# One-hot tiles of a gate-matrix builder: from four tokens innermost to one token after the other

## The chip, the cores and the metric

The kernel runs on one core of a Trainium2 chip. The metric is the device time of one execution, in microseconds (us). A profiled execution also leaves a trace of all five engines: TensorE (PE, with its weight loads listed apart as PEld), VectorE (DVE), ScalarE (ACT), GpSimd (POOL) and SyncE (SP, which issues most DMAs).

## The reference, cut to what matters

One layer of a decoder: three gated branches (dilated attention, a convolution module, attention into a memory), then a mixer called PEER that retrieves single-neuron experts. The prompt has 1024 tokens, the sample batch 8. Per token and head, PEER takes the best 16 of 128 keys on each of two sides, sums the pairs, and keeps 16 experts of the 128 x 128, so a token has 8 x 16 = 128 slots, each with a pair of indices and a softmax weight:

```
e = take_along_axis(i1, ci // 16) * 128 + take_along_axis(i2, ci % 16)
g = softmax(sc)
a = einsum('bd,bed->be', xb, u_tab[e])
out = einsum('be,bed->bd', g * gelu(a), v_tab[e])
```

## The kernel before, in words

The 1024 prompt tokens are treated in two ways. For the first 640 (five blocks of 128) the kernel runs all 16384 experts densely: it computes gelu(h u) for every expert and multiplies by a matrix G that holds the softmax weight where the token chose the expert and zero elsewhere. For the last 384 tokens and the samples it gathers the chosen rows of the tables by indirect DMA (`peer_gather`) and works on DVE.

The stages in order of the program: memory keys; `front(0)` (projections, attention, convolution and gates of the first 512 tokens); `tail` "0" (output projection, norm, top-k); then `front(1)` for the second 512 tokens, into which the G matrices of blocks 0 to 3 are woven by `gate_build`; the tails "1a" and "1b", with the G matrix of block 4 woven in; and last `peer_dense`, with the gather running beside it on POOL, the DMA queues and DVE.

`gate_build` makes G as a product of one-hots. A block's indices and weights are transposed, so that slots lie on the 128 partitions and tokens along the free dimension (`igT`). They are converted to f16 in the tile `ig`, whose four planes are first index, second index, weight times 16384, and what the rounding of that weight left over. Per batch of 8 tokens (TB = 8) DVE runs four operations of 1024 f16 elements: `o1` (first index equal to 0..127), `o2` (second index equal to 0..127), `wh` = o1 times weight, and `wl` = o1 times remainder, written over o1. In the trace and in the order all of them are called `oh`, on lines L1047, L1048, L1049 and L1051. Per token PE then runs two 128 x 128 matmuls into the PSUM tile `pG`: o2 is the stationary operand, wh (L1056) and wl (L1057) the moving one. Four tokens share a pG tile; ACT copies it into the staging tile `stg` (L1058), and after 32 tokens one DMA stores stg (`gscr`). There are 80 batches, 320 DVE operations, 160 pG tiles and 1280 matmuls.

Memory layout before: a one-hot tile is [128 partitions, TB/4, 128, 4], so the four tokens of a group lie side by side and the 128 elements of one token lie four elements (8 bytes) apart. The constant `iotaT` repeats each of 0..127 four times. So DVE reads all operands in runs of four neighbours, and PE reads its operands of one token with a step of four elements.

Every engine executes its instructions in the order of its queue. The order is made before the run by a scheduler that places instructions by priority and by an estimate of their durations. `gate_build` gets its priorities spread over `front(1)` (`prio0 + step * prio_step`), so its work is filled in between the matmuls of that stage. The one-hot tiles have two buffers per name, pG two, stg two, ig one.

Of the kernel before, what the change touches and what calls it, by code (L numbers as in the profile page):

```python
# [12 lines left out]
F16 = mybir.dt.float16  # L13
# [3 lines left out]
OP = mybir.AluOpType  # L17
# [4 lines left out]
P = 128  # L22
# [13 lines left out]
GSCALE = 16384.0  # L36
# [10 lines left out]
def peer_trunk(tc, I, O):  # L47
    nc = tc.nc
# [10 lines left out]
    with contextlib.ExitStack() as es:  # L59
# [12 lines left out]
        bkeep = es.enter_context(tc.tile_pool(name="bkeep", bufs=1, side="right"))  # L72
# [21 lines left out]
        def cload(name, shape, src=None, pool=None):  # L94
            t = (pool or const).tile(shape, F32, name=f"c_{name}", tag=f"c_{name}")
            prio = tc.cur_priority
            tc.cur_priority = prio + 300
            nc.sync.dma_start(t, I[name] if src is None else src)
            tc.cur_priority = prio
            return t  # L100
# [23 lines left out]
        iota = cload("iota", [P, P])  # L124
        iota16 = const.tile([P, TOPK], BF16, name="iota16", tag="iota16")
        nc.vector.tensor_copy(iota16, iota[:, 0:TOPK])
        iotaT = bkeep.tile([P, P, 4], F16, name="iotaT", tag="iotaT")
        nc.vector.tensor_copy(iotaT, iota.unsqueeze(2).to_broadcast([P, P, 4]))
        blk = cload("blk", [P, NS])
        sel = cload("sel", [32, NS])  # L130
        subk = cload("sub_keys", [P, 2, P])
# [15 lines left out]
        igT = {b: igp.tile([P, 3, P], F32, name=f"igT{b}") for b in range(4)}  # L147
# [868 lines left out]
        def gate_build(gb, pgs, toks, TB, prio0=None, prio_step=0):  # L1016

            step = 0
            for t0 in range(toks[0], toks[1], TC):
                bi = t0 // P  # L1020
                if t0 % P == 0:
                    pt = pgs.tile([P, 4, P], F32, tag="pG", bufs=2, name=f"igT{bi}")
                    for q in range(3):
                        nc.tensor.transpose(pt[:, q], igT[bi][:, q], ident)
                    nc.scalar.copy(igT[bi], pt[:, 0:3])
                    ig = gb.tile([P, 4, P], F16, tag="ig", bufs=2 if TB == 16 else 1, name=f"ig{bi}")
                    nc.vector.tensor_copy(ig[:, 0:2], igT[bi][:, 0:2])
                    nc.vector.tensor_scalar(ig[:, 2], igT[bi][:, 2], GSCALE, None, op0=OP.mult)
                    nc.vector.scalar_tensor_tensor(
                        ig[:, 3], igT[bi][:, 2], GSCALE, ig[:, 2], op0=OP.mult, op1=OP.subtract  # L1030
                    )
                stg = gb.tile([P, P, TC], F32, tag="stg", bufs=2, name=f"stg{t0}")
                for tb in range(0, TC, TB):
                    ts_ = slice(t0 % P + tb, t0 % P + tb + TB)
                    if prio0 is not None:
                        tc.cur_priority = prio0 + step * prio_step
                        step += TB // 4
                    o1, o2, wh = (
                        gb.tile([P, TB // 4, P, 4], F16, tag=f"oh{q}", bufs=2, name=f"oh{q}_{t0}_{tb}") for q in range(3)
                    )  # L1040
                    ioB = iotaT.unsqueeze(1).to_broadcast([P, TB // 4, P, 4])

                    def cols(q):
                        c = ig[:, q, ts_].rearrange("p (a t) -> p a t", t=4)
                        return c.unsqueeze(2).to_broadcast([P, TB // 4, P, 4])

                    nc.vector.tensor_tensor(o1, ioB, cols(0), op=OP.is_equal)  # L1047
                    nc.vector.tensor_tensor(o2, ioB, cols(1), op=OP.is_equal)  # L1048
                    nc.vector.tensor_tensor(wh, o1, cols(2), op=OP.mult)  # L1049
                    wl = o1  # L1050
                    nc.vector.tensor_tensor(wl, o1, cols(3), op=OP.mult)  # L1051
                    for t4 in range(0, TB, 4):
                        pG = pgs.tile([P, 4, P], F32, tag="pG", bufs=2, name=f"pG{t0}_{tb + t4}")
                        for t in range(t4, t4 + 4):
                            a, q = t // 4, t % 4
                            nc.tensor.matmul(pG[:, q], o2[:, a, :, q], wh[:, a, :, q], start=True, stop=False)  # L1056
                            nc.tensor.matmul(pG[:, q], o2[:, a, :, q], wl[:, a, :, q], start=False, stop=True)  # L1057
                        nc.scalar.activation(  # L1058
                            stg[:, :, tb + t4 : tb + t4 + 4], pG.rearrange("p t i -> p i t"), AF.Copy, scale=1.0 / GSCALE
                        )  # L1060
                nc.sync.dma_start(gscr[t0 // TC], stg)
# [66 lines left out]
        with tc.tile_pool(name="keep", bufs=1) as keep, tc.tile_pool(name="wts", bufs=1) as wp:  # L1128
            mem_stage(wp)
            mg = front(0, keep, wp)  # L1130
            p0 = tc.cur_priority + 2200
            tail("0", keep, wp, *mg, [(b * P, P, b * P) for b in range(4)] + [(HALF, NS, SEQ)])
            tc.cur_priority = p0
            phase.update(mm=3, o=1, g=2)
            with tc.tile_pool(name="psG", bufs=1, space=PSUM) as pgs:
                base = tc.cur_priority
                with tc.tile_pool(name="gb0", bufs=1, side="right") as gb:
                    gate_build(gb, pgs, (0, HALF), 8, base, 20)
                tc.cur_priority = base
                mg = front(1, keep, wp)  # L1140
                fes.close()
                gp = es.enter_context(tc.tile_pool(name="gath", bufs=1, side="right"))
                base = tc.cur_priority
                tc.cur_priority = base + low_prio
                peer_gather(gp, [gp], [NGB])
                gprio, tc.cur_priority = tc.cur_priority, base
                with (
                    tc.tile_pool(name="igp1", bufs=1, side="right") as igp1,
                    tc.tile_pool(name="topk1", bufs=1, side="right") as kp,
                    tc.tile_pool(name="gb1", bufs=1, side="right") as gb,  # L1150
                ):
                    igT[4] = igp1.tile([P, 3, P], F32, name="igT4")
                    tail(
                        "1a", keep, wp, *mg, [(b * P, P, HALF + b * P) for b in (0, 1)],
                        after=lambda b: gate_build(gb, pgs, (b * P, b * P + P), 8), kpool=kp,
                    )
                    tail("1b", keep, wp, *mg, [(b * P, P, HALF + b * P) for b in (2, 3)], kpool=kp)
# [88 lines left out]
```

## Time and profile before

| what | value |
|---|---|
| time, median of three runs | 3703.09 us (3703.05 to 3704.65) |
| profiled execution | 3695.24 us |
| its span, first to last instruction | 3693.1 us |
| PE matmul busy | 3429.9 us (93%) |
| PE weight loads busy | 3011.5 us (82%) |
| DVE busy | 2899.1 us (78%) |
| ACT busy | 1499.6 us (41%) |
| POOL busy | 565.7 us (15%) |
| mean granted TensorE clock | 0.961 of full speed |

Busy shares are averages over the whole span. The gate matrices of blocks 0 to 3 are built from about 1020 to 1500 us and that of block 4 from about 1725 to 1832 us; the dense stage follows to the end. Matmul records overlap (a matmul's record is longer than the time until the next one starts), so the time that a matmul costs in a row of matmuls is read from the starts of neighbours, not from the record's length.

### The profile page before, as it was taken

How to read it: one execution, taken by the hardware profiler on the slowest of the kernel's cores; microseconds unless marked ns; L12 is line 12 of the kernel's file. 1: busy time of each engine (PE TensorE's matmuls, PEld its weight loads, DVE VectorE, ACT ScalarE, POOL GpSimd, SP SyncE). 2: the span in 40 equal slices, each digit the busy share in tenths (PEclk: the TensorE clock that was granted, in tenths of full speed). 3: DMA queues.
4: the chain of work that ended last, by engine and by line, in shares of the span. 5: the costliest groups of instructions: out<-in, count | busy, mean ns of one | idle time of the engine just before them, and what ended most of it. 6: DMA issues, size and time to landing. Idle time of an engine off the chain costs nothing.

```text
span 3693.1 us, 55182 instructions
## 1 busy us (share of the span) xinstructions
PE 3429.9 (93%) x19969; PEld 3011.5 (82%) x19969; DVE 2899.1 (78%) x6275; ACT 1499.6 (41%) x3519; POOL 565.7 (15%) x398
## 2 busy tenths in 40 slices
PE   8987999898889989887899999999999999999998
PEld 6766989697677778676798888888989888898987
DVE  4358555499998656779988888887988888798988
ACT  6553552235755554344443333332333333233332
POOL 0000000000000000000012323322323332233332
PEclk9997999999999999998799999999999999999999
DMA  5467455423355546753668988888988988888987
GB/s 180 136 199 259 154 184 183 154 86 119 103 186 189 177 157 211 246 188 131 224 233 314 338 312 330 310 318 309 336 328 324 342 315 304 308 327 318 334 329 279
DMA packets 338454, 902.09 MB, mean 244 GB/s; under 512 B 32588, under 2 KB 140276, under 8 KB 285436
## 3 DMA queue, kind: packets, MB, share of 16 engines
q1 hardware_dynamic: 281732, 487.49, 39.7%
q0 software_dynamic: 56448, 411.07, 29.2%
q8 instruction: 157, 2.57, 0.3%
q14 instruction: 117, 0.96, 0.1%
HBM read 804.09 MB, written 94.83 MB: 243 GB/s over the span
## 4 chain that ended last, share of the span: by engine, by line
PE 31%; issue 30%; DVE 14%; DMA 13%; POOL 11%; ACT 2%; SPq 0%; POOLq 0%; DVEq 0%; ACTq 0%
POOL uv L981 11%; DMA uv<-in_uv,idxB 4%; PE pg L175 2%; PE pg L174 2%; PE pg L176 2%; PE pG L1057 2%; PE pG L1056 2%; DMA vr<-in_v_tab 1%; PE p_q L175 1%; PE p_q L176 1%; DMA wko<-kscr 1%; PE p_q L174 1%; DMA uv<-in_uv,idxS 1%; PE pa L174 1%; PE pa L176 1%
## 5 line engine op out<-in xcount | busy, mean ns | idle before, releaser
L981 POOL DMA_INDIRECT uv<-in_uv,idxB x384 | 555.8, 1448 | 1553.2 <-DVE gacc L995 1226.1
L174 PE MATMUL pa<-h2Ah,uh 128*128 128x320 f32 x2048 | 633.7, 310 | 2.2 <-ACT uh L158 2.2
L176 PE MATMUL pa<-h2Ah,ul 128*128 128x320 f32 x2048 | 631.9, 310 | 2.3 <-DVE ul L159 2.2
L175 PE MATMUL pa<-h2Al,uh 128*128 128x320 f32 x2048 | 633.2, 309 | 0.0
L985 DVE CUSTOM_DVE_ANT_0 uv<-uv,gh 128x1024 f32<-128x1024 f32 x392 | 478.5, 1222 | 138.2 <-DMA uv<-in_uv,idxB 119.9
L174 PE MATMUL pv<-vh,hh 128*128 128x512 f32 x1280 | 480.5, 396 | 44.3 <-ACT vh L158 28.4
L995 DVE SCALAR_TENSOR_TENSOR gacc<-uv,av,gacc 128x1024 f32<-128x1024 f32 x392 | 502.5, 1282 | 17.5 <-ACT av L993 12.6
L175 PE MATMUL pv<-vl,hh 128*128 128x512 f32 x1280 | 505.2, 395 | 9.3 <-DVE vl L159 9.3
L176 PE MATMUL pv<-vh,hl 128*128 128x512 f32 x1280 | 499.9, 393 | 0.0
L174 PEld LDWEIGHTS pa<-h2Ah,uh 128*128 128x128 f32 x2048 | 385.7, 188 | 6.9 <-ACT uh L158 2.4
L176 PEld LDWEIGHTS pa<-h2Ah,ul 128*128 128x128 f32 x2048 | 385.1, 188 | 5.4 <-DVE ul L159 2.8
L175 PEld LDWEIGHTS pa<-h2Al,uh 128*128 128x128 f32 x2048 | 385.4, 188 | 3.3 <-issue 0.9
L158 ACT CAST vh<-vr 128x512 fp32r<-128x512 f32 x256 | 157.2, 619 | 422.0 <-DMA vr<-in_v_tab 238.1
L174 PEld LDWEIGHTS pv<-vh,hh 128*128 128x128 f32 x1280 | 242.7, 190 | 99.0 <-ACT vh L158 40.0
L175 PEld LDWEIGHTS pv<-vl,hh 128*128 128x128 f32 x1280 | 243.6, 190 | 61.0 <-DVE vl L159 12.9
L176 PEld LDWEIGHTS pv<-vh,hl 128*128 128x128 f32 x1280 | 243.4, 190 | 50.0
L981 POOL DMA_INDIRECT uv<-in_uv,idxS x8 | 9.2, 1149 | 1556.3 <-ACT co L739 1513.2
L159 DVE TENSOR_TENSOR vl<-vr,vh 128x512 fp32r<-128x512 f32 x256 | 175.6, 688 | 77.0 <-ACT vh L158 76.5
L174 PE MATMUL pg<-hTh,wh_g 128*128 128x260 f32 (+1 forms) x576 | 192.9, 335 | 0.0
L175 PE MATMUL pg<-hTl,wh_g 128*128 128x260 f32 (+1 forms) x576 | 192.4, 334 | 0.0
L176 PE MATMUL pg<-hTh,wl_g 128*128 128x260 f32 (+1 forms) x576 | 192.3, 334 | 0.0
L990 ACT ACTIVATE av<-av 128x2 f32<-128x2 f32 x196 | 39.9, 204 | 375.3 <-DVE av L985 374.8
(558 smaller groups left out, 7651.3 us busy)
## 6 DMA issues: line engine op xcount, KB each, us to landing
ur<-in_uT SPq DMA_DIRECT2D x128, 512.0 KB
vr<-in_v_tab SPq DMA_DIRECT2D x256, 256.0 KB
gscr<-stg SPq DMA_DIRECT2D x20, 2048.0 KB
Gt<-gscr SPq DMA_DIRECT2D x32, 1280.0 KB
wr_g<-in_w_col SPq DMA_DIRECT2D x48, 512.0 KB
wr_q<-in_w_in SPq DMA_DIRECT2D x24, 512.0 KB
wr_u<-in_w_col SPq DMA_DIRECT2D x16, 512.0 KB
wr_pq<-in_w_col SPq DMA_DIRECT2D x16, 512.0 KB
```

Source lines behind the costliest of these rows:

```text
L158: nc.scalar.copy(hi, raw)
L159: nc.vector.tensor_tensor(lo, raw, hi.bitcast(F32), op=OP.subtract)
L174: nc.tensor.matmul(out, ah, bh, start=start, stop=False)
L175: nc.tensor.matmul(out, ah, bl, start=False, stop=False)
L176: nc.tensor.matmul(out, al, bh, start=False, stop=stop)
L981: nc.gpsimd.indirect_dma_start(out=uv, out_offset=None, in_=I["uv"], in_offset=bass.IndirectOffsetOnAxis(ap=col, axis=0),)
L985: nc.vector.tensor_tensor_reduce(out=uv[:, 0:D], in0=uv[:, 0:D], in1=h2, scale=1.0, scalar=0.0, op0=OP.mult, op1=OP.add, accum_out=av[:, s ...
L990: nc.scalar.activation(av, av, AF.Gelu_apprx_tanh)
L995: nc.vector.scalar_tensor_tensor(acc, uv[:, D:], av[:, j : j + 1], acc, op0=OP.mult, op1=OP.add)
L1056: nc.tensor.matmul(pG[:, q], o2[:, a, :, q], wh[:, a, :, q], start=True, stop=False)
L1057: nc.tensor.matmul(pG[:, q], o2[:, a, :, q], wl[:, a, :, q], start=False, stop=True)
```

## The change

One-hot tiles become [128 partitions, TB, 64, 2]: each token's 128 elements lie side by side, split into 64 pairs only so that an operand can be described in pairs. `ig` now holds every value twice in a row, and its two values are read 64 times per token; `iotaT` becomes plain 0..127, read once per token. The conversion into `ig` was one cast of two planes, one scaled copy and one subtraction; it is now two casts (one per plane), one scaled copy and one subtraction, each of 256 elements where a plane had 128. PE reads its operands without a step. Number, size and operands of the one-hot operations, matmuls and evacuations are as before.

```
-        iotaT = bkeep.tile([P, P, 4], F16, name="iotaT", tag="iotaT")
-        nc.vector.tensor_copy(iotaT, iota.unsqueeze(2).to_broadcast([P, P, 4]))
+        iotaT = bkeep.tile([P, P], F16, name="iotaT", tag="iotaT")
+        nc.vector.tensor_copy(iotaT, iota)
...
-                    ig = gb.tile([P, 4, P], F16, tag="ig", bufs=2 if TB == 16 else 1, name=f"ig{bi}")
-                    nc.vector.tensor_copy(ig[:, 0:2], igT[bi][:, 0:2])
-                    nc.vector.tensor_scalar(ig[:, 2], igT[bi][:, 2], GSCALE, None, op0=OP.mult)
+                    ig = gb.tile([P, 4, P, 2], F16, tag="ig", bufs=1, name=f"ig{bi}")
+
+                    def twice(q):
+                        return igT[bi][:, q].unsqueeze(2).to_broadcast([P, P, 2])
+
+                    for q in range(2):
+                        nc.vector.tensor_copy(ig[:, q], twice(q))
+                    nc.vector.tensor_scalar(ig[:, 2], twice(2), GSCALE, None, op0=OP.mult)
...
-                        gb.tile([P, TB // 4, P, 4], F16, tag=f"oh{q}", bufs=2, name=f"oh{q}_{t0}_{tb}") for q in range(3)
-                    )
-                    ioB = iotaT.unsqueeze(1).to_broadcast([P, TB // 4, P, 4])
+                        gb.tile([P, TB, P // 2, 2], F16, tag=f"oh{q}", bufs=2, name=f"oh{q}_{t0}_{tb}") for q in range(3)
+                    )
+                    shape = [P, TB, P // 2, 2]
+                    ioB = iotaT.rearrange("p (a e) -> p a e", e=2).unsqueeze(1).to_broadcast(shape)
 
                     def cols(q):
-                        c = ig[:, q, ts_].rearrange("p (a t) -> p a t", t=4)
-                        return c.unsqueeze(2).to_broadcast([P, TB // 4, P, 4])
+                        return ig[:, q, ts_].unsqueeze(2).to_broadcast(shape)
...
-                            a, q = t // 4, t % 4
-                            nc.tensor.matmul(pG[:, q], o2[:, a, :, q], wh[:, a, :, q], start=True, stop=False)
-                            nc.tensor.matmul(pG[:, q], o2[:, a, :, q], wl[:, a, :, q], start=False, stop=True)
+                            a, h, l = (x[:, t].rearrange("p a e -> p (a e)") for x in (o2, wh, wl))
+                            nc.tensor.matmul(pG[:, t - t4], a, h, start=True, stop=False)
+                            nc.tensor.matmul(pG[:, t - t4], a, l, start=False, stop=True)
```

The scheduler's order follows the changed operations. On DVE, at the start of the gate matrix of block 0, stood before (ig is the converted tile, the names with `oh_0_0` and `oh_0_8` are the one-hots of the first two batches):

```order
L1027 CAST ig_9783<-igT_133 128x256
L1028 TENSOR_SCALAR ig_9783<-igT_133 128x128
L1047 TENSOR_TENSOR oh_0_0_9788<-iotaT,ig_9783 128x1024
L1048 TENSOR_TENSOR oh_0_0_9789<-iotaT,ig_9783 128x1024
L1029 SCALAR_TENSOR_TENSOR ig_9783<-igT_133,ig_9783 128x128
L1047 TENSOR_TENSOR oh_0_8_9815<-iotaT,ig_9783 128x1024
L1048 TENSOR_TENSOR oh_0_8_9816<-iotaT,ig_9783 128x1024
L154 RECIPROCAL rstd<-rstd 128x4
L1049 TENSOR_TENSOR oh_0_0_9790<-oh_0_0_9788,ig_9783 128x1024
```

At the same place of DVE's queue stands now (lines are five further down in the changed file):

```order
L1032 CAST ig_9783<-igT_133 128x256 x2
L1033 TENSOR_SCALAR ig_9783<-igT_133 128x256
L1052 TENSOR_TENSOR oh_0_0_9789<-iotaT,ig_9783 128x1024
L1052 TENSOR_TENSOR oh_0_8_9816<-iotaT,ig_9783 128x1024
L1053 TENSOR_TENSOR oh_0_0_9790<-iotaT,ig_9783 128x1024
L1053 TENSOR_TENSOR oh_0_8_9817<-iotaT,ig_9783 128x1024
L154 RECIPROCAL rstd<-rstd 128x4
L1034 SCALAR_TENSOR_TENSOR ig_9783<-igT_133,ig_9783 128x256
```

One cast more, three operations twice as long, the subtraction a few places later; the one-hots are the same eight operations.

On PE, in the stage `front(1)`, where the first attention transposes (wT, of keys wkp and wko) meet the convolution's projection (pu) and the fourth batch of one-hots, stood before:

```order
L175 MATMUL pu_14340<-hTl_11576,wh_u_14329 128x512
L176 MATMUL pu_14340<-hTh_11575,wl_u_14330 128x512
L174 MATMUL pu_14340<-hTh_11575,wh_u_14329 128x512
L380 MATMUL wT_12901<-ident,wkp_12891 128x128
L175 MATMUL pu_14340<-hTl_11576,wh_u_14329 128x512
L176 MATMUL pu_14340<-hTh_11575,wl_u_14330 128x512
L380 MATMUL wT_12901<-ident,wko_12893 128x128
L1057 LDWEIGHTS oh_0_24_9870
L1057 MATMUL pG_24_9876<-oh_0_24_9869,oh_0_24_9870 128x128
```

and stands now:

```order
L174 MATMUL pu_14344<-hTh_11579,wh_u_14333 128x512
L175 MATMUL pu_14344<-hTl_11580,wh_u_14333 128x512
L380 MATMUL wT_12905<-ident,wkp_12895 128x128
L380 MATMUL wT_12905<-ident,wko_12897 128x128
L1062 LDWEIGHTS oh_0_24_9871
L1062 MATMUL pG_24_9877<-oh_0_24_9870,oh_0_24_9871 128x128
```

The gate matmuls come three matmuls of 512 columns earlier here. Up to this place PE's queue is the same in both programs, but for the numbers in names; behind it neighbours swap places in the same way through the rest of `front(1)`, the tails and, less often, the dense stage. POOL's order is the same.

## Rows read from the trace of the kernel before

**Rows 1.** Busy time (count) of PE, PEld, DVE, ACT, POOL by stretch; clock, DMA.

```profile
1018.00:1200.00 182.00, 167.71 (x1001) 139.12 (x999) 163.41 (x302) 97.42 (x237) 0.00 (x0) 0.94 0.53 186
1200.00:1500.00 300.00, 281.27 (x1652) 236.59 (x1651) 191.73 (x370) 149.59 (x325) 0.00 (x0) 0.95 0.53 183
1725.00:1832.00 107.00, 88.20 (x654) 81.85 (x653) 107.00 (x357) 47.48 (x86) 6.10 (x4) 0.83 0.53 185
1832.00:3693.00 1861.00, 1799.16 (x9980) 1630.88 (x9978) 1579.52 (x2192) 600.80 (x1349) 549.74 (x380) 0.99 0.86 315
```

**Rows 2.** Same stretches, pG instructions alone: PE busy (count), ACT busy (count).

```profile
1018.00:1200.00 182.00, 56.14 (x402) 29.55 (x50) 0.94 0.53 186
1200.00:1500.00 300.00, 84.14 (x622) 46.16 (x78) 0.95 0.53 183
1725.00:1832.00 107.00, 35.10 (x256) 18.98 (x32) 0.83 0.53 185
```

**Rows 3.** Same stretches, oh instructions alone: PE, PEld, DVE busy (count).

```profile
1018.00:1200.00 182.00, 56.14 (x402) 45.37 (x402) 70.77 (x108) 0.94 0.53 186
1200.00:1500.00 300.00, 84.14 (x622) 69.04 (x622) 96.43 (x148) 0.95 0.53 183
1725.00:1832.00 107.00, 35.10 (x256) 28.66 (x256) 43.10 (x64) 0.83 0.53 185
```

**Rows 4.** Chain of waits, shares by line, first 1018 to 1500, then 1725 to 1832.

```profile
by line: PE pG L1057 10.9%; PE pG L1056 10.7%; PE pg L176 8.4%; PE pg L174 8.3%; PE pg L175 8.3%; DMA wko<-kscr 6.7%; DMA wkp<-kscr 4.3%; PE wo L332 3.9%; PE pS_w L319 3.6%; PE wT L380 3.4%; PE pu L176 3.1%; PE pu L174 3.1%; PE pu L175 3.1%
by line: PE pq1b L174 7.4%; PE pq1b L176 6.9%; PE pq1b L175 6.9%; PE pG L1057 5.5%; DVE oh L1051 5.2%; DVE oh L1047 5.0%; DVE oh L1049 5.0%; PE pG L1056 4.9%; DVE oh L1048 4.6%; DVE mr1b L849 4.4%; DVE ix1b L848 4.2%; DMA ur<-in_uT 4.2%; DV
```

**Rows 5.** What DVE waited for, 1018 to 1500: total, times, longest.

```profile
DVE oh L1047 <- PE pG L1057: 59.2, 35, 8.4
```

**Rows 6.** PE timeline: start, length in us; gate matmuls back to back.

```profile
1028.67 0.30 PE L1056 MATMUL pG<-oh,oh 128*128 128x128 f16 x1
1028.79 0.30 PE L1057 MATMUL pG<-oh,oh 128*128 128x128 f16 x1
1028.91 0.30 PE L1056 MATMUL pG<-oh,oh 128*128 128x128 f16 x1
```

**Rows 7.** PE timeline, matmuls of 512 columns, 256 columns, and small stationaries.

```profile
1019.95 0.39 PE L174 MATMUL pu<-hTh,wh_u 128*128 128x512 f32 x1
1020.19 0.39 PE L175 MATMUL pu<-hTl,wh_u 128*128 128x512 f32 x1
1020.41 0.40 PE L176 MATMUL pu<-hTh,wl_u 128*128 128x512 f32 x1
...
1720.32 0.28 PE L175 MATMUL pq1b<-h2l1b,wh_pq1b 128*128 128x256 f32 x1
1720.44 0.28 PE L176 MATMUL pq1b<-h2h1b,wl_pq1b 128*128 128x256 f32 x1
...
512.71 1.93 PE L532 MATMUL spam<-svm,PTm 128*8 128x128 f32 x64
```

**Rows 8.** Groups by line: count, busy us, mean ns, idle before and releaser.

```profile
L1056 PEld LDWEIGHTS <-oh 128*128 128x128 f16 x640 | 74.5, 118 | 28.8 <-issue 19.8 <-DVE oh L1049 4.8 <-DVE y L575 0.8
L175 PEld LDWEIGHTS pq<-h2l,wh_pq 128*128 128x128 f32 x256 | 48.6, 190 | 0.0
L1058 ACT ACTIVATE stg<-pG 128x512 f32<-128x512 f32 x160 | 94.7, 599 | 101.5 <-PE pG L1057 100.7
L1049 DVE TENSOR_TENSOR oh<-oh,ig 128x1024 f16<-128x1024 f16 x80 | 55.2, 694 | 0.0
L159 DVE TENSOR_TENSOR ul<-ur,uh 128x1024 fp32r<-128x1024 f32 x128 | 156.6, 1223 | 34.5 <-ACT uh L158 34.4
```

**Rows 9.** Groups by line and shape, DVE: short operations and short runs.

```profile
L1027 DVE CAST ig<-igT 128x256 f16<-128x256 f32 x5 | 1.5, 294 | 3.7 <-ACT igT L1025 3.0 <-DMA egs<-iq 0.6
L911 DVE TENSOR_TENSOR oh<-oh 128x512 bf16<-128x512 bf16 x8 | 3.4, 431 | 0.0
L911 DVE TENSOR_TENSOR oh<-oh 128x256 bf16<-128x256 bf16 x8 | 3.3, 417 | 0.0
```

**Rows 10.** Tile pa, the first matmuls of the dense stage: first and last start.

```profile
L174 PE MATMUL pa<-h2Ah,uh x2048: 303/309/472, 1828.2 to 3666.7; 128*128 128x320 f32 x187
```

More of the change, by code (lines that the diff above doesn't have):

```diff
@@ L1025, in gate_build @@
                     nc.scalar.copy(igT[bi], pt[:, 0:3])
-                    ig = gb.tile([P, 4, P], F16, tag="ig", bufs=2 if TB == 16 else 1, name=f"ig{bi}")
-                    nc.vector.tensor_copy(ig[:, 0:2], igT[bi][:, 0:2])
-                    nc.vector.tensor_scalar(ig[:, 2], igT[bi][:, 2], GSCALE, None, op0=OP.mult)
+                    ig = gb.tile([P, 4, P, 2], F16, tag="ig", bufs=1, name=f"ig{bi}")
[4 more added lines that the diff above has]
+                    nc.vector.tensor_scalar(ig[:, 2], twice(2), GSCALE, None, op0=OP.mult)
                     nc.vector.scalar_tensor_tensor(
-                        ig[:, 3], igT[bi][:, 2], GSCALE, ig[:, 2], op0=OP.mult, op1=OP.subtract
+                        ig[:, 3], twice(2), GSCALE, ig[:, 2], op0=OP.mult, op1=OP.subtract
                     )
```

## The prediction

> **What bounds the kernel now.** I first read the busy time by stretch, because the change touches two stretches only. In the stage that builds the gate matrices of blocks 0 to 3, PE is busy 167.7 of 182 us and then 281.3 of 300 us, DVE 163.4 and 191.7 [rows 1]. So the first part has two engines near full and the second has PE alone. While block 4 is built (1725 to 1832) DVE has no idle time at all and PE has 19 us of it [rows 1]. The dense stage from 1832 on is PE's: 1799 of 1861 us [rows 1]. Its first matmul starts at 1828.2 [rows 10], and from there the work is the same in both kernels, so what is gained ahead of it should come out at the end.
>
> Next I read the same stretches for the gate matmuls alone: 402, 622 and 256 of them, 1280 in all [rows 2]. Then the chain of waits: from 1018 to 1500 the two lines of gate matmuls are 10.9% and 10.7% of it, the largest entries; from 1725 to 1832 they are 5.5% and 4.9%, and the rest is mostly DVE and other matmuls [rows 4]. DVE itself waits 59.2 us in the first stage for gate matmuls to free a one-hot buffer [rows 5]. So in that stage PE's time on gate matmuls is time of the kernel, and DVE mostly waits for PE.
>
> **The step of a gate matmul.** Back to back, gate matmuls start 0.12 us apart (1028.67, .79, .91) [rows 6]; I count 0.118, the length of their weight load's record, which fills the step [rows 8]; 1024 of them make 121 us of PE in the first stage. For 128 columns that is long: matmuls with 256 columns and no step between elements also start 0.12 apart, and 512 columns 0.23 apart [rows 7]. A line through these two, 0.11 us for 256 columns more, gives 0.065 us at 128 columns.
>
> Can something other than the step of four elements hold it at 0.118? Issue: 64 pairs of a weight load of 8 columns and a matmul of 128 take 1.93 us, 0.03 us a pair [rows 7], so issuing a pair is no limit. (These run in four column groups side by side; they are the lowest end, not the value.) Weight loads: the gate's record is 118 ns, that of the 256-column matmuls 190 ns [rows 8], and the latter hides under a step of 0.12 us; a load with the shorter record should hide under less. What is left is the moving operand's reading, and that is what the change makes contiguous. The trace has no contiguous f16 matmul, so the bounds are 0.03 and 0.118 us, and I take 0.065, the line through the rows that read contiguously. That is 0.053 us less per matmul: 21.3 us (402), 33.0 us (622) and 13.6 us (256).
>
> [...]
>
> **What of it is time.** 1018 to 1200: without 21.3 us PE needs 146 us, DVE still 163.4 plus about 2 for the conversions below. An engine that sets the pace here reaches the share that PE has in the dense stage, 1799/1861 = 0.967. So the stretch ends near 165.4/0.967 = 171 us: 11 us gained, not 21. 1200 to 1500: DVE has 108 us of room. Of the gate matmuls' 121 us in both parts, (0.109 + 0.107) x 482 = 104 us lie on the chain, 86%; the rest passes beside waits for attention loads, which stay (wko 6.7%, wkp 4.3% [rows 4]). 0.86 x 33.0 = 28 us. 1725 to 1832: PE's 13.6 us buy nothing, since DVE is full; were DVE not the bound they would be worth up to 13.6.
>
> Evacuation: ACT needs 599 ns for a pG tile [rows 8] and PE 8 x 0.118 = 0.94 us to fill one, after the change 8 x 0.065 = 0.52. In a long run ACT would become the pace, 0.08 us a tile. Runs seldom exceed two tiles, because DVE needs 4 x 0.694 = 2.8 us for the two tiles of a batch, and pG has two buffers; that cover holds. Without it 128 tiles x 0.08 = 10 us would go.
>
> **The one-hots on DVE.** The four operations of a batch keep 1024 elements; only the innermost run of `ig` falls from four to two, read 64 times over. They take 694 ns now, a 1024-element operation on 4-byte data 1223 [rows 8]; so f16 goes two at a time. The ends are 694 and 1223, and I take 694, since operands stay 2 bytes wide in neighbouring runs. One row is a warning: a bf16 operation on runs of two takes 417 ns for 256 elements where runs of four take 431 for 512 [rows 9]. There each run lies 32 bytes from the next, here the pairs follow each other or repeat, so I read it as the cost of the gaps.
>
> [...] By the 417 ns row alone they would lose the double rate. [...]
>
> **Conversions and order.** Per block one cast, one scaled copy and one subtraction become four operations of 256 elements. Against a cast of 256 at 294 ns [rows 9], each costs at most about 0.3 to 0.45 us, together some 0.5 us more than now: 2 us on DVE in the first stage, 0.5 in the full stretch of block 4, where it counts. The plain `iotaT` saves less than 0.3 us near the start, beside PE work. The new order swaps neighbours and adds no wait; I give it 5 us either way, in the range only.
>
> **Sum.** 11 + 28 - 0.5 = 38.5, say 39 us off. The profiled execution took 3695.24 us (span 3693.1 and 2.1 around it), so one like it would take 3656. The median of the runs shown is 3703.09, 7.9 us above it; against that the forecast is 3664 us.
>
> **Rivals.** *The gain is half eaten.* PE falls to 0.065 but the attention loads and ACT end last where gate matmuls did; for it speak 11% of the chain in those loads and the idle PE they leave [rows 4], against it that PE is 94% busy in the second stretch [rows 1]. Half of the gain is left: 3683.
>
> *The step of a matmul does not change*, because reading every fourth element costs nothing over reading neighbours, or because the weight load of 128 columns holds it at 0.118 whatever the layout (its record is as long as the step [rows 6, 8]). Then only the conversions' 0.5 us count: 3704. [...]
>
> *Slower: the one-hots lose their double rate.* With runs of two at 1223 ns each operation costs 529 ns more: 108 of them are 57 us in the first stretch, 148 are 78 us in the second, 64 are 34 us in the full one [rows 3]. First stretch: (163.4 + 57 + 2)/0.967 = 230, 48 longer than now; second: (191.7 + 78)/0.967 = 279 against 300, so PE's gain there falls to 21; third: 34 longer. 3703 + 48 - 21 + 34 = 3764. For it speaks the 417 ns row. It decides from where DVE's cost meets the 39 us: each ns per operation adds 0.108/0.967 + 0.064 = 0.176 us, so from 0.22 us, an operation of about 0.92 us.
>
> **Chances.** Forecast 0.62 (3648 to 3680 by itself: a step between 0.03 and 0.08 us, and the order), half eaten 0.16, step unchanged 0.13, one-hots slower 0.09. Faster by over 0.2% (7.4 us, about what a measurement can tell from none): 0.62 + 0.15 + 0.02 = 0.79. Within it: nearly all of the third case and a little of the second, 0.12. Slower: 0.09. The range reaches from 3640 (all 54 us of the first stage gained, and 9 of block 4's) to 3703, which takes in the second case and half of the third; the slower case stays outside.
>
> **What the new profile would show.** Gate matmuls starting 0.06 to 0.08 us apart, with one-hots at 690 to 700 ns, and the first dense matmul near 1790 in place of 1828. PE busy on gate matmuls in the first stage falling well below 140 us, DVE's wait for them (59.2 us) shrinking, and DVE at some 97% up to about 1190. Wrong: starts still 0.12 apart (step), one-hot operations above 0.9 us (DVE), or the dense stage earlier and the end not (then the order of that stage, or the gather, has become the bound).

## The result, and the profile after

Over 14 executions each, on one chip, the kernel before has a median of 3703.79 us and the changed kernel 3678.88 us: a ratio of 0.993, 95% interval 0.991 to 0.9949. Two later comparisons gave 0.9947 (0.9928 to 0.9966) and 0.9945 (0.9928 to 0.9961). So the change saves 19 to 25 us; the forecast was 39 (3664 us). The time lies inside the range, but most of the missing 14 to 20 us have a cause, the new order of instructions, that the forecast had put at 5 us at most.

The profiled execution of the changed kernel took 3687.05 us (span 3685.3). Single executions of either kernel lie up to 16 us from their median here, so the end of one pair of traces proves little; starts and waits inside it do.

First the timeline of PE (start and length in us), gate matmuls in a row, against [rows 6]:

```profile
1033.09 0.22 PE L1062 MATMUL pG<-oh,oh 128*128 128x128 f16 x1
1033.15 0.22 PE L1061 MATMUL pG<-oh,oh 128*128 128x128 f16 x1
1033.20 0.22 PE L1062 MATMUL pG<-oh,oh 128*128 128x128 f16 x1
```

They start 0.05 to 0.06 us apart (0.057 in a long row) where it was 0.12. The same groups of the page as in [rows 8] (busy us, mean ns of one, idle before):

```profile
L1061 PEld LDWEIGHTS <-oh 128*128 128x128 f16 x640 | 63.5, 102 | 31.6 <-issue 16.5 <-DVE oh L1054 10.1 <-DVE y L575 1.4
L1063 ACT ACTIVATE stg<-pG 128x512 f32<-128x512 f32 x160 | 89.4, 598 | 58.2 <-PE pG L1062 57.3
L1054 DVE TENSOR_TENSOR oh<-oh,ig 128x1024 f16<-128x1024 f16 x80 | 54.5, 685 | 0.0
```

A one-hot takes 685 ns (694 before), an evacuation 598 (599). Busy time by stretch, as in [rows 1] (PE, PEld, DVE, ACT, POOL, clock, DMA), and below it the pG instructions alone (PE, ACT), as in [rows 2]:

```profile
1018.00:1200.00 182.00, 153.23 (x1025) 123.21 (x1024) 170.09 (x325) 99.47 (x258) 0.00 (x0) 0.92 0.54 188
1200.00:1500.00 300.00, 276.79 (x1757) 223.84 (x1756) 212.20 (x427) 156.64 (x344) 2.29 (x2) 0.97 0.62 212
...
1018.00:1200.00 182.00, 33.84 (x418) 28.59 (x52) 0.92 0.54 188
1200.00:1500.00 300.00, 45.66 (x606) 42.85 (x76) 0.97 0.62 212
```

The same 1024 gate matmuls keep PE busy for 79.5 us instead of 140.3, and DVE is the fuller engine of the first part (170.1 of 182). The waits, over the whole run (total, times, longest), the first of which answers to [rows 5]:

```profile
DVE oh L1052 <- PE pG L1062: 22.3, 17, 7.7
PE pG L1061 <- ACT stg L1063: 6.1, 11, 2.1
```

DVE waits 22 us for PE, no longer 59; PE now waits 6.1 us for ACT's evacuation. The chain of waits from 1018 to 1500, as in [rows 4]:

```profile
by line: DMA wko<-kscr 8.7%; PE pg L175 6.7%; PE pg L174 6.7%; PE pg L176 6.7%; DMA wkp<-kscr 6.5%; issue 5.2%; PE pG L1061 4.0%; PE pG L1062 3.7%; PE wT L380 3.6%; PE wo L332 3.5%; PE pS_w L319 3.4%; DMA wvo<-vscr 3.1%; PE pu L174 2.5%; PE
```

Gate matmuls fell from 21.6% to 7.7% of the chain, and the loads of keys (wko, wkp) lead it. The dense stage, as in [rows 10]:

```profile
L174 PE MATMUL pa<-h2Ah,uh x2048: 302/309/633, 1792.1 to 3666.8; 128*128 128x320 f32 x187
```

Its first matmul comes at 1792.1, 36 us earlier than before, and its last at 3666.8, no earlier than before. That was the sign named in advance for "the order of that stage, or the gather, has become the bound", and the experiments had to tell which.

### The profile page after: what moved, and what is told of

The parts are those of the page before. It is cut to its first block, busy times and chain, and to the rows that moved or that the text cites. A ratio compares the mean times of both kernels' runs of the same rounds, so it can differ in the third digit from the quotient of the medians.

```text
span 3685.3 us, 55180 instructions
## 1 busy us (share of the span) xinstructions
PE 3371.1 (91%) x19969; PEld 2953.3 (80%) x19969; DVE 2904.0 (79%) x6280; ACT 1492.0 (40%) x3519; POOL 565.3 (15%) x398
## 4 chain that ended last, share of the span: by engine, by line
PE 29%; issue 28%; DVE 16%; DMA 15%; POOL 9%; ACT 3%; SPq 1%; POOLq 0%; DVEq 0%; ACTq 0%
POOL uv L981 9%; DMA uv<-in_uv,idxB 5%; PE pg L175 2%; PE pg L174 2%; PE pg L176 2%; DMA vr<-in_v_tab 1%; PE pv L174 1%; PE pv L175 1%; PE pv L176 1%; DMA wko<-kscr 1%; PE pa L176 1%; PE pa L174 1%; PE pa L175 1%; PE p_q L175 1%; DVE gacc L995 1%
## 5 line engine op out<-in xcount | busy, mean ns | idle before, releaser
L158 ACT CAST uh<-ur 128x1024 fp32r<-128x1024 f32 x128 | 134.2, 1049 | 182.0 <-PE pa L175 139.1
```

What stands on the lines that cost most here:

```text
L158: nc.scalar.copy(hi, raw)
```

## The experiments

All ratios are to the kernel before, on the same chip, with 95% intervals.

**The changed kernel again.** No edit.

> The changed kernel unaltered, for a second trace of the same order. In the first pair of traces the dense stage (from the first dense matmul to the end of the span) took 1864.9 us before and 1893.2 us after, so 28 of the 36 us that the changed kernel gained up to its first dense matmul were gone at the end of that execution. Theory A (the new order of the dense stage costs it): the dense stage is again 1885 to 1900 us long. Theory B (its length differs from execution to execution, because gathers, table loads and DVE meet by chance): a length anywhere between 1860 and 1895. First dense matmul near 1792 by both; time about 3679, 0.993 of the kernel before.

3673.95 us against 3692.58, ratio 0.9947 (0.9928 to 0.9966). First dense matmul at 1790.3, dense stage (from there to the end of the span) 1880.4 us. That is longer than the 1864.9 of before and 13 us shorter than in the first trace; it lies just under the range named for A and inside that for B, so this run alone does not decide between an offset and a scatter.

**Which operand makes the step, and what is it worth?** The changed kernel, with PE reading every fourth element of the same tiles, so that G holds wrong values; the order of all engines is the changed kernel's to the last instruction.

```
+ s0, q4 = t // 4 * 4, t % 4
+ a = o2[:, s0 : s0 + 4].rearrange("p t a e -> p (t a e)").rearrange("p (i q) -> p i q", q=4)[:, :, q4]
- a = o2[:, t].rearrange("p a e -> p (a e)")
  (the same for h of wh and l of wl; in the other two kernels only a, or only h and l)
```

> The changed kernel with one thing altered: PE reads 128 elements that lie four apart from the same one-hot tile (stationary and moving operand), as before the change, so G holds wrong values. Order of every engine, DVE's work and all sizes are those of the changed kernel. My theory: the reading alone makes the step, so gate matmuls start 0.118 us apart again, the first dense matmul comes 36 to 40 us later (about 1830) and the time is 3679 + 39 = 3718 if the dense stage of this order is the longer one (theory A), or 3704 if it is not (theory B). Rival (the gain came from the new order or from DVE's layout, not from PE's reading): time stays at 3679 and the first dense matmul at 1792.

> As the kernel with both operands read four apart, but only the stationary operand (weight load) is; the moving one is contiguous; G holds wrong values. My theory (the moving operand's reading set the step): starts stay at 0.057 us, time at 3679. Rival (the weight load set it; its record fell from 118 to 98 ns): starts 0.118 us, first dense matmul near 1830, 3704 to 3718 us. If each holds a part: in between.

> As above with only the moving operand read four apart and the stationary one contiguous; G holds wrong values. My theory: starts 0.118 us apart, weight load records 98 ns, first dense matmul near 1830, time 3704 to 3718. Rival (the weight load sets the step): starts 0.057 us, time 3679.

Both operands: 3711.62 us, 1.0049 (1.003 to 1.0067). Stationary alone: 3671.72, 0.9947 (0.9926 to 0.9967). Moving alone: 3711.46, 1.0043 (1.0026 to 1.0061). Timelines of PE, first the stationary, then the moving operand read with the step:

```profile
1030.01 0.22 PE L1064 MATMUL pG<-oh,oh 128*128 128x128 f16 x1
1030.07 0.22 PE L1065 MATMUL pG<-oh,oh 128*128 128x128 f16 x1
1030.12 0.22 PE L1064 MATMUL pG<-oh,oh 128*128 128x128 f16 x1
```

```profile
1032.07 0.30 PE L1065 MATMUL pG<-oh,oh 128*128 128x128 f16 x1
1032.18 0.29 PE L1064 MATMUL pG<-oh,oh 128*128 128x128 f16 x1
1032.30 0.29 PE L1065 MATMUL pG<-oh,oh 128*128 128x128 f16 x1
```

The moving operand alone sets the step: 0.057 us against 0.117 with the moving operand strided. A strided stationary lengthens the weight load's record (shortest from 94 to 110 ns, median from 98 to 113) and no step: the load hides. With only the moving operand strided the median record is 115 ns, not the 98 that was expected, though its shortest is still 94: the median grew here with the matmuls' step as well. On one and the same order the reading is worth 3711.6 - 3674.0 = 37.7 us. And the kernel with both strided is 19 us *slower than before*, though PE reads as before: that is what the rest of the change (order and conversions) costs. The conversions of a block take 1.29 us on DVE instead of 0.80, about 0.5 us more as forecast, so nearly all of the 19 us is order.

**The old order with contiguous reading.** The kernel before; PE takes 128 neighbours of the old tile, so G holds wrong values. The order is that of before to the last instruction.

```
- nc.tensor.matmul(pG[:, q], o2[:, a, :, q], wh[:, a, :, q], start=True, stop=False)
+ a, h, l = (x[:, t // 4].rearrange("p e t -> p (e t)")[:, q * P : (q + 1) * P] for x in (o2, wh, wl))
+ nc.tensor.matmul(pG[:, q], a, h, start=True, stop=False)
```

> The kernel before with one thing altered: PE reads 128 neighbours of the old tile (four tokens innermost) as stationary and moving operand, so G holds wrong values. The order of all engines and DVE's work are those of before. Theory: reading and order are two separate terms. On the changed kernel's order contiguous reading was worth 3711.6 - 3674.0 = 38 us, and with strided reading the changed kernel's order was 19 us slower than before. So this kernel: 38 us under the kernel before, ratio 0.990 (about 3655 where before has 3692.6), 19 us under the changed kernel, dense stage near 1865 us from its first matmul to the end. Rival: whatever starts the dense stage earlier makes it longer (gathers, tables and DVE in the way), whatever the order: dense stage 1880 to 1894, ratio 0.995, no faster than the changed kernel.

3663.37 us against 3695.61, ratio 0.9915 (0.9895 to 0.9934). Busy times over the first 30 us and the whole of the dense stage, first before, then old order and contiguous reading, changed order and strided reading, changed order and contiguous reading (the second trace of the changed kernel):

```profile
1828.20:1858.20 30.00, 30.00 (x194) 29.44 (x195) 28.65 (x140) 14.63 (x20) 0.00 (x0) 0.94 0.84 270
1828.20:3693.10 1864.90, 1802.96 (x10002) 1634.58 (x10002) 1583.32 (x2206) 603.23 (x1353) 549.74 (x380) 0.99 0.86 315
```

```profile
1795.00:1825.00 30.00, 29.68 (x192) 28.87 (x193) 29.29 (x141) 14.51 (x20) 0.00 (x0) 0.94 0.86 279
1795.00:3660.10 1865.10, 1803.95 (x10002) 1637.29 (x10002) 1584.29 (x2208) 605.09 (x1353) 548.58 (x380) 0.98 0.86 315
```

```profile
1828.60:1858.60 30.00, 22.03 (x125) 20.89 (x126) 30.00 (x163) 10.56 (x14) 0.00 (x0) 0.83 0.60 195
1828.60:3711.30 1882.70, 1806.14 (x10020) 1639.61 (x10020) 1588.26 (x2211) 605.88 (x1355) 556.63 (x380) 0.98 0.85 312
```

```profile
1790.30:1820.30 30.00, 20.50 (x132) 19.33 (x133) 30.00 (x158) 10.95 (x15) 0.00 (x0) 0.83 0.60 196
1790.30:3670.70 1880.40, 1803.23 (x10020) 1637.85 (x10020) 1589.85 (x2214) 605.90 (x1355) 547.69 (x380) 0.98 0.85 312
```

The stage's length goes with the order (1865 or 1881), not with when it starts: the first and the third kernel start it at 1828, the second and the fourth at 1790 to 1795. PE's busy time in it is 1803 to 1806 us in all four; what differs is idle PE. In the first 30 us it is 8 and 9.5 us in the changed order, at most 0.3 in the old one. The conversions are over by then, and nearly all one-hots, so what is left as a cause is the order.

**Two tokens innermost.** The kernel before with the four tokens of a group replaced by two; a version meant to keep the order and lose the step.

```
- gb.tile([P, TB // 4, P, 4], F16, tag=f"oh{q}", bufs=2, ...)
+ gb.tile([P, TB // 2, P, 2], F16, tag=f"oh{q}", bufs=2, ...)
- a, q = t // 4, t % 4
+ a, q = t // 2, t % 2
  (iotaT, ioB and cols likewise in runs of two; pG[:, t - t4] for pG[:, q])
```

> The kernel before with two tokens innermost instead of four (tile of 128 partitions, 4 pairs, 128 elements, 2 tokens; right values): DVE reads runs of two, conversions and order of every engine are those of before, PE reads with a step of two elements (4 bytes). If PE's step goes with the bytes between elements in proportion: starts about 0.077 us apart (0.057 at step one, 0.118 at four), 26 us gained, ratio 0.993. If reading every second f16 element costs nothing over neighbours: starts 0.057, 38 us gained, ratio 0.990, faster than the changed kernel by 19 us because the order stays. If any step costs the same: starts 0.118, ratio 1.000. One-hots on DVE at 686 to 694 ns by all; 1223 if a run of two with neighbouring tokens loses double rate (then over 1.01).

3662.36 us against 3695.61, ratio 0.9917 (0.9896 to 0.9937); its order is that of before to the last instruction. Its gate matmuls:

```profile
1028.33 0.22 PE L1057 MATMUL pG<-oh,oh 128*128 128x128 f16 x1
1028.38 0.22 PE L1056 MATMUL pG<-oh,oh 128*128 128x128 f16 x1
```

Every second f16 element is read as fast as neighbours (0.057 us); every fourth takes twice as long (0.117 us). The granted clock of TensorE is 1.00 where neighbours take 0.057 us (1033.0 to 1033.6 us of the changed kernel) and where every fourth takes 0.118 (1028 to 1030 us of the kernel before). At 0.50, the other level in the trace, every second and every fourth differ by 0.01 us. Two stretches at that level, first of the kernel before, where PE had waited up to 2.1 us at a time for attention loads, then of two innermost, where it had waited 7.6 us (in the first row of each, the third number from the end is the granted clock):

```profile
1147.40:1149.20 1.80, 1.80 (x17) 1.73 (x16) 0.62 (x2) 1.33 (x3) 0.00 (x0) 0.50 0.07 27
1147.50 0.31 PE L1057 MATMUL pG<-oh,oh 128*128 128x128 f16 x1
1147.62 0.30 PE L1056 MATMUL pG<-oh,oh 128*128 128x128 f16 x1
```

```profile
1316.30:1318.00 1.70, 1.70 (x16) 1.65 (x15) 0.00 (x0) 0.60 (x1) 0.00 (x0) 0.50 0.25 106
1316.35 0.31 PE L1057 MATMUL pG<-oh,oh 128*128 128x128 f16 x1
1316.46 0.31 PE L1056 MATMUL pG<-oh,oh 128*128 128x128 f16 x1
```

With a granted clock of 0.50, starts are 0.12 us apart with the step of four, as at 1.00, and 0.11 with the step of two (0.119 and 0.108 on average over all such stretches of the stage). So the step of four costs 0.06 us a matmul at 1.00 and 0.01 at 0.50. One-hots stay at 686 ns, dense stage 1869.6 us. Because order and conversions are those of before, this kernel also gives the cleanest account of the gain by stage (below).

**What losing the double rate costs.** Contiguous tokens, with the index read once per token and repeated 128 times with step zero, and the three conversions of before.

```
- ig = gb.tile([P, 4, P, 2], F16, ...)
+ ig = gb.tile([P, 4, P], F16, ...)
- shape = [P, TB, P // 2, 2]
+ shape = [P, TB, P]
```

> The changed kernel with the three conversions of before and index and weight read once per token and repeated 128 times with step zero innermost, tile of 128 partitions, 8 tokens, 128 elements (right values; the order is a third one). It prices the rival by which one-hots lose their double rate: if an operand repeated with step zero halves the rate, one-hots take 1223 ns and the time is near the rival's 3764 (ratio about 1.017 to 1.02); if not, they stay at 686 ns and the time is that of the changed kernel, 0.99 to 1.0 by the order. Gate matmuls start 0.057 us apart when one-hots are there by both.

3802.38 us, ratio 1.0298 (1.0274 to 1.0323). A group of its page:

```profile
L1049 DVE TENSOR_TENSOR oh<-oh,ig 128x1024 f16<-128x1024 f16 x80 | 97.9, 1227 | 0.0
```

The rate falls by nearly half (1227 ns an operation, 685 in the changed kernel), to the upper end given for it (1223 ns). The doubled `ig` of the change is what avoids this.

**The order of the dense stage alone.** The changed kernel, the dense stage's priority raised.

```
- tc.cur_priority = base
+ tc.cur_priority = base - 3000
```

> The changed kernel with the dense stage's priority 3000 steps higher, nothing else: PE's order is the same up to the entry of the dense stage and differs in 1478 places behind it (right values). On ACT the first gelu still stands behind the softmax of tail 1b, with one more one-hot evacuation between. Theory (the order of the dense stage sets its length): the first dense matmul stays near 1790 and the dense stage takes another length than 1880 to 1894; the direction is open, the 8 us of idle PE at its entry stay. Rival (length set by the early start): 1880 to 1894 again, time 3674 to 3679.

3691.55 us against 3695.61, ratio 0.9995 (0.9975 to 1.0015); first dense matmul at 1786.5, dense stage 1900.2 us. Nothing but a reordering from the entry of that stage on, and the gain is gone within noise: 4 us under the kernel before, where the changed kernel is 19 to 25 under it. PE's idle time in the first 30 us did not stay at 8 us but grew to 11.8.

**The two best side by side.** No edits.

> The kernel with two tokens innermost again, side by side with the changed kernel on one chip. Theory (its matmuls are as fast as contiguous ones and it keeps the order of before): dense stage 1862 to 1872 us again, ratio to before about 0.992, some 10 to 19 us under the changed kernel. Rival (its first result was a lucky execution): no faster than the changed kernel, dense stage above 1875.

> The changed kernel for the comparison with the kernel of two tokens innermost: ratio to before 0.993 to 0.995 and a dense stage of 1880 to 1894 us by the theory that its order costs time there; below 1872 would speak for chance.

3661.34 and 3674.74 us against 3697.01: 0.9897 (0.9871 to 0.9924) and 0.9945 (0.9928 to 0.9961). The kernel with two tokens innermost is 13.4 us faster than the changed one. Dense stages: 1866.8 and 1881.4.

## Why the prediction was right in sign and too large

**The step: right, a little low.** Forecast 0.065, measured 0.057, against the bounds 0.03 and 0.118. The moving operand's reading set it and the weight load hides, as argued. That the weight load's record is as long as the step was a coincidence: with a strided stationary alone it is 113 ns, and the step 0.057 us. With the moving operand's f16 elements 8 bytes apart the step was 0.117 us, with 4 bytes apart and contiguous 0.057.

**The gain ahead of the dense stage: 34 for 39.** The kernel with two tokens innermost and the one before share their order, so the same instruction can be compared; up to 1016 they are 0.2 us apart.

| instruction (start, us) | before | two innermost | gained |
|---|---|---|---|
| last p_qm, ahead of the gate work | 1016.3 | 1016.1 | 0.2 |
| ACT tg, near 1200 | 1201.03 | 1189.81 | 11.2 |
| last pg, end of `front(1)` | 1512.4 | 1479.3 | 33.1 |
| first pa, dense stage | 1828.2 | 1794.2 | 34.0 |

Busy times between these marks, before and then with two innermost:

```profile
1018.00:1201.00 183.00, 168.71 (x1009) 140.05 (x1008) 164.41 (x303) 98.35 (x238) 0.00 (x0) 0.94 0.53 186
1201.00:1512.00 311.00, 292.27 (x1698) 245.40 (x1697) 199.91 (x406) 153.81 (x336) 0.00 (x0) 0.96 0.54 186
```

```profile
1018.00:1189.80 171.80, 151.18 (x1014) 120.50 (x1014) 163.69 (x304) 95.28 (x238) 0.00 (x0) 0.93 0.57 198
1189.80:1479.00 289.20, 262.15 (x1691) 214.30 (x1691) 199.04 (x405) 149.87 (x336) 0.00 (x0) 0.94 0.58 201
...
1690.00:1794.00 104.00, 76.92 (x647) 70.05 (x646) 104.00 (x351) 45.04 (x85) 6.08 (x4) 0.87 0.51 185
```

- *1018 to 1200, forecast 11: 11.2.* DVE took over as said, 163.7 of 171.8 us, a share of 0.953 for the 0.967 assumed.
- *1200 to 1500, forecast 28: 22.* Here a term was mis-sized. PE loses 30.1 us of busy time, but its idle time grows from 18.7 to 27.1. Its waits for loads of keys (wkp, wko) grow from 14.5 to 19.5 us, those for other loads by 1.4, and 1.9 us of waiting for evacuation come in. "0.86 of PE's saving" took the share of the chain as the share that goes when the work goes; it was 22 of 33, 0.66.
- *Block 4, forecast 0: 0.9.* DVE has no idle time in it (104.00 of 104) before and after.
- *Evacuation, forecast no cost.* PE waits 6.1 us for it in the changed kernel, 4.6 with two innermost: the cover held for all but a few tiles, within the 10 us named.
- *One-hots on DVE, forecast 694 ns.* 685. The rival's price was low: at 1227 ns per one-hot the kernel takes 107 us more than before, not 61; that kernel also has a third order, and how much of the other 46 us that is was not tried.

**The step that failed: "the new order swaps neighbours and adds no wait; I give it 5 us either way", and with it "what is gained ahead of it should come out at the end".** The work of the dense stage is the same, its order is not. Its length is 1864.9, 1865.1, 1869.6 and 1866.8 us in four traces of the old order (mean 1866.6), and 1893.2, 1880.4, 1882.7, 1893.9, 1879.7 and 1881.4 in six of the changed order, whichever operand was strided (mean 1885.2): 18.6 us. A few of these are only an earlier first matmul: in the kernels that read fast it comes at 1787.7 to 1793.1 in the changed order and at 1794.2 to 1800.2 in the old one. In times, the changed order costs 19.0 us where PE reads with the step (3711.6 against 3692.6) and 13.4 where it reads neighbours or every second element (3674.7 against 3661.3, side by side). So the two ways from before to the changed kernel meet: 32.2 us off for the reading (3695.6 to 3663.4) and then 13 back for the order, or 19.0 on and then 37.7 off. Both give about 19; the two later comparisons measured 18.6 and 22.3.

Where the time goes can be read in two places. The first is the entry. SyncE's queue, the last store of gate matrices and the first load of them, before and then in the changed kernel (second trace; first dense matmul 1828.2 and 1790.3):

```profile
1831.56 0.33 SPq L1061 DMA_DIRECT2D gscr<-stg  x1
...
1839.67 3.40 SPq L1089 DMA_DIRECT2D Gt<-gscr  x2
```

```profile
1805.48 0.33 SPq L1066 DMA_DIRECT2D gscr<-stg  x1
...
1812.77 4.23 SPq L1094 DMA_DIRECT2D Gt<-gscr  x2
```

Before, the last store is issued 3.4 us behind the first dense matmul; now 15.2 us behind it (3.4 to 4.1 in the four traces of the old order, 14.4 to 15.6 in the six of the changed one). The first gelu on ACT waits for that store to land: the trace of the kernel before names it (first fence). In the changed kernel the wait is listed as "issue", but it ends in the same moment as SyncE's wait for the store, at 1812.77 (second fence):

```profile
1839.71 0.77 ACT L1102 ACTIVATE ge<-pa 128x320 f32<-128x320 f32 x2 [0.59 <-DMA gscr<-stg]
```

```profile
1804.38 1.07 ACT L1063 ACTIVATE stg<-pG 128x512 f32<-128x512 f32 x2
...
1812.77 1.28 ACT L1107 ACT_TABLE_LOAD   x1 [5.69 <-issue]
1814.07 1.09 ACT L1107 ACTIVATE ge<-pa 128x320 f32<-128x320 f32 x3
```

PE has filled its pa tiles by then and stands still for ACT; its longest wait in the same 30 us:

```profile
PE pa L174 <- ACT ge L1107: 6.5, 1, 6.5
```

So the dense stage was let in early, and block 4's gate matrices, which have to be stored first, came out late. Idle PE here was 7 to 9.5 us in all six traces of the changed order, and at most 0.3 in the four of the old one. So the first dense matmul, which the forecast took for the stage's begin, overstates the gain: 9 of its 36 us come back at once as idle PE.

The second place is the middle. From 800 to 1400 us into the stage PE idles 20.9 us before and 36.3 in the changed kernel (second trace); it is 17 to 21 in the four traces of the old order and 29 to 38 in the six of the changed one:

```profile
2628.20:3228.20 600.00, 579.12 (x3210) 525.68 (x3210) 502.18 (x653) 191.62 (x439) 186.41 (x127) 0.99 0.88 322
```

```profile
2590.30:3190.30 600.00, 563.70 (x3152) 513.40 (x3152) 490.18 (x635) 188.22 (x431) 179.01 (x124) 0.97 0.86 316
```

PE's waits for the cast of v rows (vh) in the same two stretches (total, times, longest):

```profile
PE pv L174 <- ACT vh L158: 7.3, 4, 3.8
```

```profile
PE pv L174 <- ACT vh L158: 15.2, 3, 11.3
```

They come to 15 to 28 us in the six traces of the changed order, with a single one of 10.4 to 11.3 in each, and to 7 to 8 in the four of the old order, where the longest is 5.3. (The wait for DVE's accumulator dacc grows in this pair too, from 8.1 to 18.1, but over all traces it scatters: 6 to 8 in the old order, 3 to 18 in the changed one.) The two places together make 25 us in this pair, more than the 15 by which the stages differ: elsewhere PE idles some 10 us less. In the trace shown it is ACT that waits for the rows, and SyncE issued their load right behind one of gate matrices (Gt, 1.28 MB):

```profile
2806.67 0.38 SPq L1094 DMA_DIRECT2D Gt<-gscr  x1
2809.15 10.53 SPq L1121 DMA_DIRECT2D vr<-in_v_tab  x1
```

```profile
2826.82 0.62 ACT L158 CAST vh<-vr 128x512 fp32r<-128x512 f32 x1 [9.20 <-DMA vr<-in_v_tab]
```

That this place in the queue is the cause was not tried and stays open. With the dense stage's priority raised the longest such wait was only 4.5 us, and that stage was the longest of all, so no single wait stands for "the order".

**What was luck.** Nothing in the forecast kept the order's cost below the gain: another order of the same kernel took nearly all of it. And the first dense matmul came near 1790 as forecast because the changed order let that stage in early; with the same reading in the old order it came at 1794 to 1800.

**The rivals.** "Half eaten" gave 3683, close to the measured time, but by attention loads and ACT; those took some 6 us, the order 13 to 19. "Step unchanged" and "one-hots slower" did not happen; what each would cost is now measured.

## What to carry to other kernels

Where an instruction list is ordered by a scheduler, a change of a few small operations is two changes: price the order as a term of its own, with both signs and a size taken from how long PE idles in the stages behind it (here 13 to 19 us against a gain of 32 to 38). To measure such a change, hold the order and alter only how an operand is read; and prefer the form of the edit that leaves the list as it was: two tokens innermost reads as fast as one (0.057 us) and kept the whole gain of the reading (0.990 to 0.992). A share of the chain of waits is no share of the gain: here 0.86 of the chain became 0.66 of the saving, because waits for loads came forward.

## What the runs showed of the hardware

A 128-column f16 matmul took 0.057 us, start to start, with a moving operand contiguous or at every second element, and 0.117 with every fourth; at a granted clock of 0.50 every second took 0.11 and every fourth 0.12. A stationary operand at every fourth element lengthened its weight load's shortest record from 94 to 110 ns, hidden: the matmuls still started 0.057 us apart. DVE's f16 operations kept their rate with runs of two (685 ns for 1024 elements), also where the pair repeats 64 times, and lost it (1227 ns) where one operand is repeated with step zero innermost.
